# One decoder block on one core: block sums of the output projection on VectorE, and an MLP norm whose row factor is left to the last norm

## The chip, the core and the metric

The kernel runs on one core of a Trainium2 chip. TensorE multiplies, VectorE and ScalarE do the elementwise work, GpSimd does a little of it early on and issues DMAs, SyncE (SP) issues most of the DMAs. DMAs are issued here from SP's, ScalarE's and GpSimd's queues; those that add to what lies at the destination (`accum_op`) all from GpSimd's. Each engine works through its own instructions in order and waits on semaphores for the others. The metric is the device time of one execution in microseconds; a profiled execution gives a trace beside it.

## What is computed

One decoder block on 1024 tokens of width 1024, in float32. The part that matters here is what follows the mixer's two branches (shortened from the reference):

```python
merged = (g_pool * einsum('bsc,cd->bsd', y_pool, w_branch_pool)
          + g_attn * einsum('bsc,cd->bsd', y_attn, w_branch_attn))
mix = einsum('bsd,de->bse', merged, w_out)
x = x + rmsnorm(mix, g_mix_post)
h2 = rmsnorm(x, g_mlp_pre)
ff = einsum('bsf,fd->bsd', square(relu(einsum('bsd,df->bsf', h2, w_up))), w_down)
x = x + rmsnorm(ff, g_mlp_post)      # rmsnorm(v, g) = v * rsqrt(mean(v*v) + 1e-6) * g, by row
```

`relu` squared is homogeneous of degree two, so a factor that a whole row of `h2` carries comes out of `ff` squared, and the last norm divides it out again except in its epsilon.

## The kernel before

**Products.** Each float32 operand is split into a rounded high part (a ScalarE cast) and the rest (a VectorE subtraction); `split` does both, and three matmuls take the place of one (`PASSES`). The large products are done as 2x2 block products by Strassen's scheme in Winograd's form: seven products instead of eight, with sums of blocks as operands. Names such as S1 to S4, A11 to A22 are blocks and block sums of the activations, B11 to B22 and Q1 to Q4 those of the weights, T1 to T4 those of the MLP's activations.

**Pool branch (loop over m = 0 to 7 at L1043).** For each channel block TensorE does 24 matmuls (`mm_fm`, L456 and L458), then `bp_mul` multiplies by the gate and adds the attention branch into the tile `zm[m]`, `bp_split` prepares the next weights, and `merged` splits one half of `zm` as A11 (m < 4) or A12. `merged` also flips signs on ScalarE (`flip`, L956), and `dma_sums` (L979 to L985) forms S1, S2, S3 and S4 in place with DMAs on GpSimd's queue that add one half tile to another. All of GpSimd's other accumulations stand in the same queue: `wo_add` (L1005) adds a block of `w_out` to a weight tile, and L1300 adds one half of an output tile to the other.

**Output projection (L1243 to L1368).** `wo_mm` runs 48 matmuls for one block product, a row block of 128 tokens at a time (t = 0 to 3, 12 matmuls each). TensorE's order is A11·B11, A12·B21, S1·Q1, S2·Q2, S4·B22, S3·Q3, A22·Q4. `s12(k)` splits a whole `zm[k]` as S2 and S1. Q1 is B11 with B12 added to it; after it is split, B22 and later B21 are added to the same tile to give Q2 and Q4. The result of row block n is the tile `ct[n]`: rows 0 to 3 are complete after S4·B22, rows 4 to 7 after A22·Q4.

**Two norms and the residual.** `out_sq`, `root(0)`, `invert(0)` and `out_scale` apply the mixer's post norm; the residual x is added by a DMA on GpSimd's queue (rows 0 to 3, L1138) or by VectorE from a loaded tile (L1140); `nc.sync.dma_start` stores the sum in `x1_dram` on SP's queue. Then `norm_sq`, `root(1)`, `invert(1)` and `norm_scale` apply the MLP's norm in place. `build_first(kt, h)` transposes 128 channels of rows 0 to 3 on TensorE (L1156) and splits them into the MLP's operands; `tr_second` and `build_second` do so for rows 4 to 7.

**MLP.** `Pairs` runs the up projection: for each pair of feature blocks `load` fetches weights, `operand(p, i)` forms and splits the operand of product i, `m1` and `m2` are the first two products, `rest` the other five. Pair p's product 1 therefore needs `operand(p, 1)`, and the call `first_kt(0)` needs `operand(0, 6)` and `operand(0, 7)`. The down projection (L1640 on) runs its products in the order 1, 5, 2, 3, 6, 7, 4, each in 8 steps of 24 matmuls (L1573); `operands` loads and splits two steps ahead, the loaded blocks lying in four buffers (`raw_tile`). `fin_sq`, `add_eps`, `rsqrt_sum` and `fin_out` are the last norm and the last residual, for rows 0 to 3 after product 6 and for rows 4 to 7 after product 4. Its x1 tiles are read from `x1_dram` by `load_x1` and `fin_out`.

**What sets the order.** Inside `tc.manual_schedule(engines=...)` the named engines keep the order in which the program calls them; up to L1304 these are TensorE, VectorE, ScalarE and GpSimd (`MANUAL`), after it only TensorE. For other engines, and SP everywhere here, a planner orders the instructions by program order and by its own estimate of when they are ready. Tiles come from pools with a fixed number of buffers; one that is full makes the next tile's first writer wait. The pool `gp` (`g32`, `gr`) has 17 buffers, `st` (`stage`) has 3, `wp` (`wslot`) has 6.

## Time and profile before

| | us |
|---|---|
| median of 3 runs (lowest, highest) | 1139.15 (1136.72, 1139.19) |
| the profiled execution | 1138.17 |
| its span, first to last instruction | 1136.4 |
| TensorE busy in it | 1103.3 |
| VectorE, ScalarE, GpSimd busy in it | 811.9, 560.1, 67.3 |
| mean granted clock of TensorE | 0.984 |

A row of the timeline gives start, duration, engine, line, operation, what is written from what is read, the shape and the count; in brackets stands the idle time before it and what ended that. A row of the windows gives the stretch and its length, then the busy time and instruction count of TensorE's matmuls, its weight loads, VectorE, ScalarE and GpSimd, then the granted clock, the DMA engines' busy share and GB/s. A row of the groups ends with busy time, mean ns of one, and idle time before. A row of the DMA issues ends with the count, the size of one and the median time from issue to landing. Durations of neighbouring VectorE instructions overlap by a little under 0.1 us, so the distance of two starts is the better price. SP and POOL rows with a queue's DMA show the issue, not the transfer.

### The profile page before, as it was taken

To read this page: it belongs to the slowest core of one execution; us is meant where nothing else is said; L and a number is where in the kernel's file an instruction comes from. 1 tells how busy PE (TensorE), PEld (TensorE's weight loads), DVE (VectorE), ACT (ScalarE), POOL (GpSimd) and SP (SyncE) were. 2 spreads that over 40 slices of the span, in tenths; PEclk is the share of its full clock that TensorE was granted. 3 is DMA by queue.
4 is the path that set the end of the run, shared out by engine and by line. 5 is a ranking of instruction groups with operands and counts; after the bars stand their busy time and mean duration, and the time that the engine had idled before them with its cause. 6 is when DMAs were issued, how large, how long until landed. Compare 5 with 4: busy or idle time off the path is not lost.

```text
span 1136.4 us, 13861 instructions
## 1 busy us (share of the span) xinstructions
PE 1103.3 (97%) x5114; PEld 913.2 (80%) x5114; DVE 811.9 (71%) x1175; ACT 560.1 (49%) x927; POOL 67.3 (6%) x124
## 2 busy tenths in 40 slices
PE   9999999999999995989899999999999999999997
PEld 8888888888888884867688888888888888888886
DVE  6578877998778753857888867575557955446896
ACT  7567665544332443678545544444444345344342
POOL 0433100000001122200000000000000000000000
PEclk9999999999999996989899999999999999999999
DMA  9616465456966777954246634353698765322662
GB/s 347 150 38 190 148 202 201 151 207 205 287 253 167 197 186 158 219 163 163 75 177 216 218 140 185 121 185 121 242 336 296 245 195 191 114 93 74 215 194 92
DMA packets 92531, 208.95 MB, mean 184 GB/s; under 512 B 9520, under 2 KB 22448, under 8 KB 92464
## 3 DMA queue, kind: packets, MB, share of 16 engines
q1 hardware_dynamic: 81072, 176.75, 46.7%
q0 software_dynamic: 5632, 11.54, 5.9%
q10 hardware_dynamic: 5760, 19.79, 4.5%
q8 instruction: 40, 0.66, 0.2%
q14 instruction: 27, 0.22, 0.1%
HBM read 147.23 MB, written 55.58 MB: 178 GB/s over the span
## 4 chain that ended last, share of the span: by engine, by line
PE 86%; DMA 4%; issue 4%; DVE 3%; ACT 2%; POOL 1%; DVEq 0%; POOLq 0%; ACTq 0%
PE mm L520 24%; PE at L520 15%; PE at L1573 14%; PE mm L1573 11%; PE mm L456 4%; PE mm L610 3%; DMA g<-g 2%; PE mm L458 2%; PE mm L192 2%; PE mm L183 2%; PE sc L183 2%; PE sc L429 1%; PE sc L360 1%; DMA qr<-in_w_o_dram 1%; DMA x_dram<-c 1%
## 5 line engine op out<-in xcount | busy, mean ns | idle before, releaser
L1573 PE MATMUL at<-ar,wh 128*128 128x512 f32 x696 | 158.7, 389 | 0.0
L1573 PEld LDWEIGHTS at<-ar,wh 128*128 128x128 f32 x696 | 130.6, 188 | 27.1
L1573 PE MATMUL mm<-ar,wh 128*128 128x512 f32 x576 | 131.0, 389 | 0.0
L1573 PEld LDWEIGHTS mm<-ar,wh 128*128 128x128 f32 x576 | 108.1, 188 | 22.5
L104 DVE TENSOR_TENSOR wh<-raw,wh 128x1024 fp32r<-128x1024 f32 x51 | 62.4, 1224 | 86.0 <-ACT wh L101 85.9
L101 ACT CAST wh<-raw 128x1024 fp32r<-128x1024 f32 x51 | 53.7, 1053 | 132.9 <-PE at L1573 55.2
L101 ACT CAST wh<-st 128x512 fp32r<-128x512 f32 (+1 forms) x104 | 65.4, 642 | 92.3 <-DVE st L499 27.5
L104 DVE TENSOR_TENSOR wh<-st,wh 128x512 fp32r<-128x512 f32 (+1 forms) x105 | 74.4, 720 | 36.2 <-ACT wh L101 33.7
L520 PE MATMUL mm<-gr,wh 128*128 128x512 f32 x333 | 81.4, 396 | 2.3 <-DVE wh L104 2.0
L520 PEld LDWEIGHTS mm<-gr,wh 128*128 128x128 f32 x333 | 63.0, 191 | 16.2 <-DVE wh L104 2.5
L520 PE MATMUL mm<-T,wx 128*128 128x512 f32 x288 | 67.4, 389 | 0.0
L520 PEld LDWEIGHTS mm<-T,wx 128*128 128x128 f32 x288 | 54.1, 188 | 11.2
L520 PE MATMUL at<-T,wx 128*128 128x512 f32 x252 | 58.9, 389 | 0.0
L520 PE MATMUL mm<-x,wh 128*128 128x512 f32 x240 | 55.3, 389 | 0.0
L520 PEld LDWEIGHTS at<-T,wx 128*128 128x128 f32 x252 | 47.3, 188 | 9.8
L520 PEld LDWEIGHTS mm<-x,wh 128*128 128x128 f32 x240 | 45.0, 188 | 9.5 <-DVE z L552 0.2
L610 PE MATMUL mm<-x,wh 128*128 128x512 f32 x192 | 47.8, 395 | 0.0
L104 DVE TENSOR_TENSOR ar<-B,ar 128x1024 fp32r<-128x1024 f32 x37 | 45.2, 1220 | 2.4 <-ACT ar L101 2.0
L610 PEld LDWEIGHTS mm<-x,wh 128*128 128x128 f32 x192 | 35.2, 188 | 7.6 <-DVE qt L104 0.2
L101 ACT CAST ar<-B 128x1024 fp32r<-128x1024 f32 x37 | 38.9, 1051 | 4.7 <-DVE B L1544 2.8
L520 PE MATMUL mm<-T,wh 128*128 128x512 f32 x147 | 38.0, 401 | 3.1 <-ACT wh L101 3.1
L520 PE MATMUL at<-gr,wh 128*128 128x512 f32 x150 | 36.6, 390 | 0.0
(430 smaller groups left out, 2218.2 us busy)
## 6 DMA issues: line engine op xcount, KB each, us to landing
raw<-f_dram SPq DMA_DIRECT2D x53, 512.0 KB, 3.6
f_dram<-g SPq DMA_DIRECT2D x28, 512.0 KB, 3.2
st<-in_w_up_dram SPq DMA_DIRECT2D x24, 512.0 KB, 4.4
B<-in_w_dn_dram SPq DMA_DIRECT2D x24, 512.0 KB, 7.3
st<-in_w_g_dram SPq DMA_DIRECT2D x18, 512.0 KB, 4.1
f_dram<-g ACTq DMA_DIRECT2D x17, 512.0 KB, 2.8
g<-spill_dram SPq DMA_DIRECT2D x16, 512.0 KB, 5.2
raw<-in_w_dn_dram SPq DMA_DIRECT2D x16, 512.0 KB, 4.7
```

Source lines behind the costliest of these rows:

```text
L101: act.copy(hi, src)
L104: eng.tensor_tensor(lo, src, f32(hi), ALU.subtract)
L183: pe.matmul(bq, xs_[k][n // 4][:, xh, n % 4 * P:(n % 4 + 1) * P], wq[k][:, h, :], start=k == 0 and j == 0, stop=k == NK - 1 and j == 2)
L192: pe.matmul(bkv_of(n), xs_[k][n // 4][:, xh, n % 4 * P:(n % 4 + 1) * P], wkv[k // 2][:, h, k % 2, :], start=k == 0 and j == 0 and not (joi ...
L360: pe.matmul(sb[:, kv, i, :nk], qt[r, qx, m * P:(m + 1) * P], kx[r, k0:k0 + nk], start=j == 0, stop=j == 2)
L429: pe.matmul(yb[:, kv], v[:, c:c + P], p[ph][:, 4 * kv:4 * kv + 4].rearrange("p i q -> p (i q)"), start=j < 2, stop=j >= len(mms) - 2)
L456: pe.matmul(bs[th], whi[:, k, :], rhs(k, hl, th), start=k == 0 and hl == 0, stop=False)
L458: pe.matmul(bs[th], wlo[:, k, :], rhs(k, 0, th), start=False, stop=k == nk - 1)
L520: pe.matmul(b, w[:, wh, kt, :], x_, start=not after and kt == 0 and j == 0, stop=kt == 3 and j == 2, skip_group_check=after)
L610: pe.matmul(b, (whi, wlo)[h][:, k, :], xr(k, xh, th), start=j == 0, stop=j == len(mms) - 1)
L1573: pe.matmul(bs[t], fo[fh][:, k2, t * P:(t + 1) * P], wo_[wh][:, k2, :], start=not after and s2 == 0 and k2 == 0 and j == 0, stop=(s2, k2) ...
```

## The change

- The block sums S1 to S4 are formed by VectorE subtractions and additions in `merged` and a new `sum4`; `dma_sums` and the sign flips in `merged` are gone. All four `s12(k)` stand ahead of A12·B21.
- The MLP norm's row factor is not applied. The mixer's post norm scales by r·r1, r1 being the first norm's factor of that row, and the residual comes in as r1·x, so `ct[n]` holds r1·x1. x is always loaded (into the pool `gp`) and added by VectorE; the tile is stored from GpSimd's queue.
- The squares of r1·x1 are taken from memory in product 5 of the down projection; `scaled_eps` forms from them the epsilon that makes the last norm exact, and 1/r1, by which ScalarE scales each x1 tile as it is read. Rows 0 to 3 are finished during product 7.
- The 32 transposes of rows 0 to 3 stand inside A22·Q4, eight behind each row block; operands of pairs 1 and 2 are formed earlier; `operand(0, 6)` and `operand(0, 7)` stand ahead of the third `build_second`, `operand(6, 2)` behind pair 4's second product.

```diff
@@ -966 +966 @@
         if m < 4:
             if m % 2 == 0:
                 s3raw.append(ga_.tile([P, 2, 512], F32, tag="ga", name=nm("s3")))
-            s3 = s3raw[m // 2][:, m % 2, :]
             Am["A11"][m] = split_half(gr, first)
-            flip(s3, second)
-            flip(second, second)
-            nc.gpsimd.dma_start(s3, first, accum_op=ALU.add)
+            dve.tensor_tensor(s3raw[m // 2][:, m % 2, :], first, second, ALU.subtract)
         else:
             k = m - 4
+            s2, s1 = zm[k][:, :512], zm[k][:, 512:]
             Am["A12"][k] = split_half(ar, first)
-            flip(first, first)
-
-    def dma_sums(m):
-        if 0 <= m - 6 < 4:
-            nc.gpsimd.dma_start(zm[m - 2][:, :512], zm[m - 6][:, :512], accum_op=ALU.add)
-        if 0 <= m - 5 < 4:
-            nc.gpsimd.dma_start(zm[m - 5][:, :512], zm[m - 5][:, 512:], accum_op=ALU.add)
-        if 0 <= m - 4 < 4:
-            nc.gpsimd.dma_start(zm[m - 4][:, 512:], zm[m][:, 512:], accum_op=ALU.add)
+            dve.tensor_tensor(s1, second, s1, ALU.subtract)
+            dve.tensor_tensor(s2, s2, s1, ALU.add)
+
+    def sum4(k):
+        first = zm[4 + k][:, :512]
+        dve.tensor_tensor(first, zm[k][:, :512], first, ALU.subtract)
 
     def wo_rows(c, h, j):
         return w_o[4 * h + 2 * c:4 * h + 2 * c + 2].rearrange("k p n -> p k n")[:, :, 512 * j:512 * j + 512]
@@ -1098 +1092 @@
 
...
+    def root(ns):
+        ms = ort[:, 1, ns]
+        dve.scalar_tensor_tensor(ms, osq[:, 0, ns], EPS, osq[:, 1, ns], ALU.add, ALU.add)
+        act.activation(ort[:, 0, ns], ms, AF.Sqrt)
+
+    def invert(ns):
+        s, ms, r, t = (ort[:, i, ns] for i in range(4))
         dve.reciprocal(r, s)
         dve.tensor_tensor(t, r, r, ALU.mult)
         dve.tensor_tensor(t, t, ms, ALU.mult)
+        dve.tensor_tensor(r, r, r1[:, ns], ALU.mult)
         dve.tensor_scalar(t, t, -0.5, 1.5, ALU.mult, ALU.add)
-        dve.tensor_tensor(orr[:, which, ns], r, t, ALU.mult)
+        dve.tensor_tensor(orr[:, ns], r, t, ALU.mult)
 
     xres = {}
 
-    def out_scale(n):
-        t = ct[n]
-        dve.scalar_tensor_tensor(t, t, orr[:, 0, n:n + 1], gpost_b, ALU.mult, ALU.mult)
-        if n < 4:
-            nc.gpsimd.dma_start(t, x[n], accum_op=ALU.add)
-        else:
-            dve.tensor_tensor(t, t, xres.pop(n), ALU.add)
-        nc.sync.dma_start(x1_dram[n], t)
-
-    def norm_scale(n):
-        act.activation(ct[n], ct[n], AF.Identity, scale=orr[:, 1, n:n + 1])
+    def load_res(n):
+        xres[n] = g32([D])
+        nc.sync.dma_start(xres[n], x[n])
+
+    def out_mul(n):
+        dve.scalar_tensor_tensor(ct[n], ct[n], orr[:, n:n + 1], gpost_b, ALU.mult, ALU.mult)
+
+    def out_add(n):
+        dve.scalar_tensor_tensor(ct[n], xres.pop(n), r1[:, n:n + 1], ct[n], ALU.mult, ALU.add)
+        nc.gpsimd.dma_start(x1_dram[n], ct[n])
         hs[n] = ct[n]
-
...
@@ -1265 +1242 @@
             Am["S1"][k] = hi[:, 512:], lo[:, 512:]
 
         b22 = [wo_raw("B22", c, stage) for c in range(2)]
-        s12(0)
-        s12(1)
+        for k in range(4):
+            s12(k)
         up.load(0)
         for t in wo_mm(bm, "A12", "B21", True):
             ct[t] = yy.tile([P, D], F32, tag="y", name=nm("c1"))
@@ -1274 +1251 @@
             if t < 2:
                 wo_split("Q1", t, q1[t], wo_tile)
                 wo_add(q1[t], "B22", t)
-            else:
-                s12(t)
-            if t == 0:
-                dma_sums(9)
+            sum4(t)
         for c in range(2):
             wo_split("B22", c, b22[c], wo_tile)
         ba = [bank("at") for _ in range(4)]
@@ -1302 +1276 @@
             Am["S3"][t] = split_half(gr, s3raw[t // 2][:, t % 2, :])
     with tc.manual_schedule(engines={mybir.EngineType.PE}):
-        load_res(0)
-        load_res(1)
+        for n in range(4):
+            load_res(n)
         for t in wo_mm(ba, "S4", "B22", True):
             dve.tensor_tensor(ct[t][:, 512:], ct[4 + t][:, :512], ba[t], ALU.add)
             out_sq(t, 1)
             if t < 2:
                 wo_split("Q4", t, q1[t], wo_tile)
+            if t == 1:
+                root(p01)
+                up.operand(1, 1)
             if t == 2:
-                root(0, p01)
+                invert(p01)
+                out_mul(0)
+                out_add(0)
             if t == 3:
-                invert(0, p01)
-                out_scale(0)
-                load_res(2)
-                root(0, p23)
-                out_scale(1)
-                load_res(3)
-                invert(0, p23)
+                root(p23)
+                out_mul(1)
+                out_add(1)
+        up.load(4)
         bm = [bank("mm") for _ in range(4)]
         for t in wo_mm(bm, "S3", "Q3"):
-            if t == 1:
-                norm_sq(0)
-                norm_sq(1)
-                out_scale(2)
-                up.load(4)
-                root(1, p01)
-            if t == 2:
-                out_scale(3)
-                load_res(4)
-                load_res(5)
-                norm_sq(2)
-                invert(1, p01)
-                norm_scale(0)
-                norm_scale(1)
-            if t == 3:
-                norm_sq(3)
-                root(1, p23)
-                invert(1, p23)
-                norm_scale(2)
-                norm_scale(3)
+            if t == 0:
+                invert(p23)
+                for n in range(4, 8):
+                    load_res(n)
             u = ct[4 + t]
             dve.tensor_tensor(u[:, 512:], u[:, 512:], bm[t], ALU.add)
             out_sq(4 + t, 1)
-        up.operand(1, 1)
-        up.operand(1, 2)
-        up.operand(2, 1)
-        up.operand(2, 2)
+            if t < 2:
+                out_mul(2 + t)
+                out_add(2 + t)
+            else:
+                up.operand(t - 1, 4 - t)
         for t in wo_mm(bm, "A22", "Q4", True):
             u = ct[4 + t]
             dve.tensor_tensor(u[:, :512], u[:, :512], bm[t], ALU.add)
             out_sq(4 + t, 0)
+            for kt in range(2):
+                build_first(t % 2 * 2 + kt, t // 2)
+            if t == 1:
+                root(p45)
+                up.operand(2, 2)
             if t == 2:
-                for kt in range(4):
-                    build_first(kt, 0)
-        root(0, p45)
-        invert(0, p45)
-        out_scale(4)
-        load_res(6)
-        out_scale(5)
-        load_res(7)
-        norm_sq(4)
-        norm_sq(5)
-        root(0, p67)
+                invert(p45)
+                out_mul(4)
+                out_add(4)
+            if t == 3:
+                root(p67)
+                out_mul(5)
+                out_add(5)
     opool.__exit__(None, None, None)
 
 
@@ -1399 +1362 @@
 
 
     with tc.manual_schedule(engines={mybir.EngineType.PE}):
-        invert(0, p67)
+        invert(p67)
+        for n in (6, 7):
+            out_mul(n)
+            out_add(n)
         up.m1(0, bank("mm"))
-        root(1, p45)
-        for kt in range(4):
-            build_first(kt, 1)
-        out_scale(6)
-        out_scale(7)
         up.m1(1, bank("mm"))
-        invert(1, p45)
-        norm_scale(4)
-        norm_scale(5)
         up.load(6)
         up.load(8)
         up.load(10)
-        norm_sq(6)
-        norm_sq(7)
-        root(1, p67)
-        invert(1, p67)
-        norm_scale(6)
-        norm_scale(7)
         up.operand(3, 1)
         up.operand(3, 2)
         up.m1(2, bank("mm"))
@@ -1441 +1393 @@
         m1_late(5)
         tr = tr_second(2)
         up.operand(6, 1)
-        up.operand(6, 2)
+        up.operand(0, 6)
+        up.operand(0, 7)
         build_second(2, *tr)
         up.m2(3)
         tr = tr_second(3)
         build_second(3, *tr)
         m1_late(6)
-        up.operand(0, 6)
-        up.operand(0, 7)
         up.m2(4)
+        up.operand(6, 2)
         for kt in range(4):
             build_last(kt)
         up.operand(0, 5)
@@ -1576 +1528 @@
 
     def fin_sq(n, dj, v):
 
-        act.activation(junk, v, AF.Square, scale=ROOT_D, accum_out=sq[:, dj, n:n + 1])
+        squared.append(act.activation(junk, v, AF.Square, scale=ROOT_D, accum_out=sq[:, dj, n:n + 1]))
...
+    squared = []
+
+    def read_x1(n, t):
+        nc.sync.dma_start(flat(t), x1_dram[n])
+        with tc.issue_after(squared[-1].ins):
+            act.activation(flat(t), flat(t), AF.Identity, scale=ort[:, 4, n:n + 1])
+        xf[n] = t
+
     def load_x1(n):
-        t = rp.tile([P, 2, 512], F32, tag="w", name=nm("xf"))
-        nc.sync.dma_start(flat(t), x1_dram[n])
-        xf[n] = t
+        read_x1(n, rp.tile([P, 2, 512], F32, tag="w", name=nm("xf")))
+
+    def square_x1(n):
+        t = flat(raw_tile())
+        nc.sync.dma_start(t, x1_dram[n])
+        act.activation(t, t, AF.Square, scale=ROOT_D, accum_out=nsq[:, n:n + 1])
+
+    def scaled_eps():
+        q = ort[:, 5, :]
+        dve.reciprocal(ort[:, 4, :], r1)
+        dve.tensor_tensor(q, r1, r1, ALU.mult)
+        dve.scalar_tensor_tensor(q, q, EPS, nsq, ALU.mult, ALU.add)
+        dve.scalar_tensor_tensor(ort[:, 6, :], q, EPS, q, ALU.mult, ALU.mult)
 
     def add_eps(ns, dj):
-        dve.tensor_scalar(sq[:, dj, ns], sq[:, dj, ns], EPS, None, ALU.add)
+        dve.tensor_tensor(sq[:, dj, ns], sq[:, dj, ns], ort[:, 6, ns], ALU.add)
 
     def fin_out(n, hv):
         if n not in xf:
-            t = stage([2, 512])
-            nc.sync.dma_start(flat(t), x1_dram[n])
-            xf[n] = t
+            read_x1(n, stage([2, 512]))
         for dj in (1, 0):
             o = xf[n][:, dj, :]
             dve.scalar_tensor_tensor(o, hv[dj][n % 4], rr[:, n:n + 1], o, ALU.mult, ALU.add)
@@ -1656 +1624 @@
             tag = "mm" if i in (5, 7) else "at"
             banks[i] = [bank(tag) for _ in range(4)]
         bs = banks[{2: 1, 3: 5}.get(i, i)]
+        if i == 5:
+            square_x1(s_)
+        if i == 7 and 1 <= s_ <= 4:
+            fin_out(s_ - 1, (c11, c12))
         if i != 4 or s_ < NS - LATE:
             down_mm(i, s_, bs, i in (2, 3), [(s_, k2, t) for k2 in range(2) for t in range(4)
                                              if (i, s_, t) != (4, NS - LATE - 1, 3)])
@@ -1701 +1673 @@
                 fin_gain(0, c11[t], u[t])
                 rsqrt_sum(rr[:, n:n + 1], sq[:, 0, n:n + 1], sq[:, 1, n:n + 1])
                 fin_out(n, (c11, v))
+        if i == 2:
+            scaled_eps()
         if i == 7:
             add_eps(slice(4, NT), 1)
             for n in range(4, NT):
@@ -1708 +1682 @@
         if i == 6:
             add_eps(slice(0, 4), 1)
             rsqrt_sum(rr[:, 0:4], sq[:, 0, 0:4], sq[:, 1, 0:4], 4)
-            for n in range(4):
-                fin_out(n, (c11, c12))
     rpool.__exit__(None, None, None)
 
 
```

More of the change, by code (lines that the diff above doesn't have):

```diff
@@ L1055, in block_kernel @@
                 merged(m - 1)
-                dma_sums(m - 1)
             if m in (4, 5):
@@ L1100, in block_kernel @@
     nsq = sp.tile([P, NT], F32, tag="nsq", name="nsq", bufs=1)
-    orr = sp.tile([P, 2, NT], F32, tag="orr", name="orr", bufs=1)
-    ort = sp.tile([P, 6, NT], F32, tag="ort", name="ort", bufs=1)
+    orr = sp.tile([P, NT], F32, tag="orr", name="orr", bufs=1)
+    ort = sp.tile([P, 7, NT], F32, tag="ort", name="ort", bufs=1)
     def out_sq(n, h):
@@ L1276, in block_kernel @@
                 wo_add(q1[t], "B22", t)
-            else:
-                s12(t)
-            if t == 0:
-                dma_sums(9)
+            sum4(t)
         for c in range(2):
```

22 lines of the change are left out of this document (2 added, 20 removed).

## The prediction

> **What bounds the kernel now.** I read the head of the page first (busy time and clock), then the waits of TensorE, then TensorE in order of time around each wait, then the engine that each wait names.
>
> ```profile
> span 1136.4 us, 13861 instructions
> PE 1103.3 (97%) x5114; PEld 913.2 (80%) x5114; DVE 811.9 (71%) x1175; ACT 560.1 (49%) x927; POOL 67.3 (6%) x124
> PE at L1095 <- ACT gr L101: 13.5, 1, 13.5
> PE at L1156 <- ACT c L1144: 5.0, 2, 4.5
> PE mm L520 <- ACT wh L101: 3.4, 2, 3.1
> PE mm L520 <- DVE wh L104: 2.0, 1, 2.0
> ```
>
> TensorE is busy for 97% of the span, so a gain can only come out of the other 33 us or out of time in which it ran slowly. The four waits shown (line, who released, total, times, longest) are nearly all the idle time in the middle of the kernel. The same places in order of time, one window for each stretch; the column after the engines is the granted clock:
>
> ```profile
> 425.66:439.15 13.49, 0.00 (x1) 0.00 (x0) 0.02 (x1) 1.09 (x2) 5.01 (x5) 0.59 0.67 113
> 439.15:445.20 6.05, 6.00 (x13) 4.29 (x14) 5.31 (x5) 3.89 (x5) 1.36 (x2) 0.51 1.00 205
> 496.86:503.20 6.34, 5.77 (x20) 4.99 (x21) 4.30 (x10) 5.61 (x12) 0.00 (x0) 0.50 0.01 3
> 551.49:559.12 7.63, 7.63 (x19) 5.30 (x20) 6.43 (x9) 3.23 (x5) 0.00 (x0) 0.59 0.39 132
> 867.80:911.32 43.52, 43.52 (x193) 36.04 (x193) 40.00 (x35) 18.21 (x21) 0.00 (x0) 1.00 0.70 234
> 517.80 6.41 PE L520 MATMUL mm<-gr,wh 128*128 128x512 f32 x27 [2.01 <-DVE wh L104]
> 551.49 2.75 PE L520 MATMUL mm<-T,wh 128*128 128x512 f32 x5 [3.08 <-ACT wh L101]
> ```
>
> After a long wait the clock stands at half for some 6 us. At full clock the row from 867.80 gives 43.52 / 192 = 0.227 us a matmul (one of the 193 begins in the next product). So a wait has two prices:
> - Q1 wait: 13.49 idle, then 13 matmuls in 6.05 instead of 2.95: 16.6 us.
> - First transposes: 5.05 idle (the wait row), then half of 5.77 busy at clock 0.50: 7.9 us.
> - Up projection, pair 3: 2.0 and a neighbour of 0.3 (the rest of the 3.4): 2.3 us. No row shows a lower clock after it.
> - Up projection, product 6 of pair 0: 3.08 idle, then 19 matmuls in 7.63 instead of 4.31: 6.4 us.
>
> Together 33.2 us, the most that this change can bring. Everything behind 559 us is TensorE back to back, and the last few us are the final norm's short chain.
>
> The largest wait, at its source: ScalarE could not cast the third row block of the sums, and GpSimd's queue shows why.
>
> ```profile
> 438.06 1.04 ACT L101 CAST gr<-g 128x1024 fp32r<-128x1024 f32 x1 [13.80 <-DMA g<-g]
> 417.87 0.87 POOL L983 DMA_DIRECT2D g<-g  x1 [6.90 <-DMA g<-g]
> 422.19 1.21 POOL L1005 DMA_DIRECT2D qr<-in_w_o_dram  x1 [2.56 <-PE mm L1095]
> 428.48 1.21 POOL L1005 DMA_DIRECT2D qr<-in_w_o_dram  x1 [5.08 <-issue]
> 434.68 0.89 POOL L983 DMA_DIRECT2D g<-g  x1 [4.06 <-issue]
> DMA to landing us min/median/max: 4.0/6.0/9.2
> ```
>
> The sum of line 983 that the cast needs is issued at 434.68, behind two weight accumulations that each hold the queue 6.3 us (422.19 to 428.48). The last row is the landing time of those accumulations (the tile qr).
>
> **The change part by part.**
>
> *Block sums on VectorE.* Gone: 16 accumulating DMAs and 12 sign flips on ScalarE. Added: 16 VectorE operations on 128x512.
>
> ```profile
> 457.41 0.68 DVE L1299 TENSOR_TENSOR c<-c,mm 128x512 f32<-128x512 f32 x1
> 458.01 0.69 DVE L104 TENSOR_TENSOR gr<-s,gr 128x512 fp32r<-128x512 f32 x1
> L1029 DVE TENSOR_TENSOR g<-g,g 128x1024 f32<-128x1024 f32 x6 | 7.4, 1226 | 0.2
> ```
>
> Successive starts are 0.60 apart, 1.14 for the wide form (1.23 less the same overlap of 0.09). Each channel block of the pool branch takes 24 matmuls, 5.44 us. VectorE's work in the fullest of them (m = 5) becomes 2.3 (gate products and sum) + 0.6 (weight split) + 1.8 (one split and two sums) + 1.1 (B11 split) = 5.8 us; it overruns by 0.4 in two blocks and recovers in the next, and the weights for the next block are split before the overrun. I take nothing; without that order it is at most 2 x 0.4.
>
> ```profile
> 401.70 0.39 PE L1095 MATMUL mm<-B11h,gr 128*128 128x512 f32 x1
> ```
>
> The last block's products end where this first output product starts, 401.7; 2.3 and 1.8 later, by 406, all sums for S1 and S2 are there, and their casts begin behind the copies of the first product, at 413. So the Q1 wait goes: -16.6 us.
>
> What is late next is Q2, because its weights are Q1's, accumulated in place after Q1 was split. If TensorE does not stop, the products (48 matmuls, 10.88 us each) start at 401.7 (A11), 412.6 (A12), 423.5 (S1), 434.3 (S2), 445.2 (S4), 456.1 (S3) and 467.0 (A22).
>
> ```profile
> 417.25 1.23 DVE L104 TENSOR_TENSOR Q1l<-qr,Q1h 128x1024 fp32r<-128x1024 f32 x1
> 442.25 1.05 ACT L101 CAST Q2h<-qr 128x1024 fp32r<-128x1024 f32 x1
> ```
>
> Q1's first split ended at 418.5; now two more block splits go ahead of it, so about 420.6. The first accumulation is issued then, the second 6.3 later at 426.9, it lands 6.0 later at 432.9, cast and subtraction take 1.05 + 1.23: 435.2. S2 reaches this half at its seventh matmul, 435.9. At the median nothing is lost; with 9.2 twice it is 420.6 + 9.2 + 9.2 + 2.3 = 441.3, a wait of 5.4 and half clock after it, 3.1: 8.5 us. ScalarE's copies and A22 casts lie between, so I take +0.5, bounds 0 to 8.5. [...]
>
> Behind it in GpSimd's queue are Q4's two accumulations (issued at 433.2 and 439.5, needed at 467), then four small ones of line 1300 from 446; the last lands near 455, before S3's first tile at 459.
>
> *Mixer norm, residual, no MLP row factor.* Gone from ScalarE, and from the chain ahead of the transposes:
>
> ```profile
> L1144 ACT ACTIVATE c<-c,orr 128x1024 f32<-128x1024 f32 x8 | 8.8, 1141 | 2.0 <-DMA x_dram<-c 1.6 <-DVE orr L1130 0.4
> L1109 ACT ACTIVATE junk_b<-c 128x1024 f32<-128x1024 f32 x8 | 8.5, 1061 | 6.6 <-DMA c<-in_x_dram 6.5
> c<-in_x_dram POOLq DMA_DIRECT2D x4, 512.0 KB, 7.0
> st<-in_x_dram SPq DMA_DIRECT2D x8, 512.0 KB, 5.1
> ```
>
> The old chain was scale, accumulate x by DMA (7.0), store, square, root, scale; the new one is scale and one multiply-add with x loaded ahead. The eight x loads (5.1 each) stay on SP but go to the 17-buffer pool, where buffers come free when S2 ends (445 us); with 6 to 10 us for the first four together they are there between 451 and 455, and row block 0 needs its own at 457. The stores of x1 leave SP for GpSimd behind line 1300, and nobody reads them before the down projection. SP's queue, in which the load for pair 3 sat behind those stores, is freed.
>
> ```profile
> 477.55 2.48 DVE L1136 SCALAR_TENSOR_TENSOR c<-c,orr,bc 128x1024 f32<-128x1024 f32 x2
> 471.90 0.16 DVE L1126 RECIPROCAL sm<-ort 128x2 f32<-128x2 f32 x1
> 472.89 1.29 DVE L1136 SCALAR_TENSOR_TENSOR c<-c,orr,bc 128x1024 f32<-128x1024 f32 x1
> 512.76 2.06 DVE L1167 SCALAR_TENSOR_TENSOR gr<-at,snk,gr 128x512 fp32r<-128x512 f32 x3
> 525.64 1.03 PE L1156 MATMUL at<-cst,c 128*128 128x128 f32 x8
> 504.62 2.89 PE L520 MATMUL mm<-gr,wh 128*128 128x512 f32 x12
> ```
>
> VectorE pays 1.24 a row block for each of the two steps, and six dependent small operations for a root (five took 472.89 - 471.90 = 1.0, so 1.2). From S4's second tile (452 us): four tile additions and one operand split 3.0, two roots 2.4, four row blocks 9.9, with S3's first two additions 1.2: 16.5, so rows 0 to 3 are ready near 468.5. The first transposes stand behind A22's first tile, at 467.0 + 2.7 = 469.7. Margin 1 us: the 7.9 go; the other end is 3 us of wait, should VectorE start late.
>
> *Order around the transposes.* All 32 transposes of rows 0 to 3 now stand in A22 (0.9 us for each eight), so A22 runs from 467 (467.5 with the Q2 wait) to 482 and the first products of pairs 0, 1, 2, 3 follow at 2.72 each (pair 0 started at 504.62 before, with half the transposes still to come): pair 3 at 490.2. VectorE is at 468.5 + four more 0.60 (two additions of S3, two operand splits) = 470.9 when it turns to A22, and then has four additions 2.4, eight build steps at 0.69 = 5.5, two roots 2.4, four row blocks 9.9, operand (2,2) 0.6: 20.8, to 491.8, and only then pair 3's subtraction, 0.6: 492.4. TensorE waits about 2.2 where it waited 2.3. Bounds: 0 if the subtraction goes ahead of row blocks 6 and 7, which nothing needs before the transposes near 500; and 9.3 if VectorE comes 4 us later still (6.2 idle and 3.1 of half clock). I take +2.2.
>
> *Product 6 of pair 0.* Its operand, late by 3.08 before, goes ahead of two transposed builds that took VectorE 4.4 us each; the displaced builds and operand (6,2) are needed only 3 to 6 us later. VectorE has no norm work left here. The 6.4 go; if operand (6,2), whose buffer is freed by pair 4's second product, is late instead, 0.6 to 3 come back.
>
> *Down projection.* Added: eight x1 loads and ScalarE squares in product 5 (1.06 and 0.19 for the readout), eight scalings by 1/r1 later (1.14 each), rows 0 to 3 finished during product 7. In product 5's window above ScalarE works 18.2 of 43.5 us, so 10 us more fit. But each step now takes two of four load buffers, so a block can be loaded two steps ahead instead of four.
>
> ```profile
> B<-in_w_dn_dram SPq DMA_DIRECT2D x24, 512.0 KB, 7.3
> raw<-f_dram SPq DMA_DIRECT2D x53, 512.0 KB, 3.6
> ```
>
> Two steps are 10.9 us; the slowest of these rows, 7.3, plus cast and subtraction, 2.3, is 9.6. It fits; I take 0.
>
> **Sum.** 1138.2 (the profiled execution; span 1136.4) - 16.6 - 7.9 - 2.3 - 6.4 + 0.5 + 2.2 = 1107.7. The median of the runs shown is 1.0 above that execution, so the forecast is 1109.
>
> **Rivals.**
> 1. *Q2's accumulations take the place of the sums.* For it: 0.7 us of slack and landings up to 9.2. Against: the queue no longer carries anything else. 8.5 instead of 0.5: 1117.
> 2. *VectorE becomes the bound in S4 to A22.* For it: it takes over 16 sums, eight residual additions and gives up nothing large there, and my margins are 1 to 2 us. Against: in the same stretch ScalarE loses 17 us, on which VectorE used to wait. 9.3 instead of 2.2: 1116.
> 3. *The sums were not what held Q1.* Then the 16.6 stay, 1125. The rows against it: cast, DMA and queue name the same transfer.
> 4. *Slower: the load buffers in product 5.* If the x1 loads and squares share the four buffers so that only one block load is in flight, a step is 7.3 + 2.3 = 9.6 instead of 5.44: 8 x 4.2 = 33 more, 1142, and more with the clock. It decides from landings above 8.6 us (10.9 - 2.3) and turns the sign when a step grows by 30 / 8 = 3.8 us. For it: the loads add 4.2 MB in 43.5 us, 96 GB/s to 234. Against: ScalarE's casts there come two steps ahead of use.
>
> **How the numbers follow.** Forecast 0.66, rival 1 0.12, rival 2 0.11, rival 3 0.03, rival 4 0.08. The predicted time is the forecast's. All waits gone is 1138.2 - 33.2 + 1.0 = 1106, and the runs shown lie up to 2.4 under their median: low end 1103. Rivals 1 and 2 with some of each other's price end at 1122. What is left out is rivals 3 and 4, about 0.1. A measurement of this kernel tells a difference from about 0.3%, 3.4 us: faster 0.90 (forecast, rivals 1 to 3, less a remainder), same 0.02, slower 0.08.
>
> **What would show it.** Right: no wait of S1 for a cast released by a DMA; no clock of 0.5 between 425 and 445; the first transposes without a wait; the first products of the pairs near 482 instead of 504; product 5 without a gap. Wrong: a wait of S2 released by the cast or split of Q2 (rival 1), waits on VectorE with that engine full from 452 to 495 (rival 2), gaps in product 5 with loads above 8.6 us (rival 4). The prediction fails if new waits add up to more than 13 us.

## The result and the profile after

The changed kernel takes 1107.77 us (median of 4 runs, 1105.71 to 1107.95) against 1138.71 for the kernel before on the same chip (4 runs, 1136.72 to 1139.19): a ratio of 0.9727, 95% interval 0.9711 to 0.9744. The forecast was 1109 in a range of 1103 to 1122.

The busy times in the head of the page of the changed kernel:

```profile
PE 1095.2 (99%) x5114; PEld 909.4 (82%) x5114; DVE 822.8 (74%) x1179; ACT 551.8 (50%) x911; POOL 54.2 (5%) x112
```

And all its waits of TensorE (line, who released, total, times, longest); the span is 1106.0 us:

```profile
PE mm L201 <- DVE pad L160: 1.1, 1, 1.1
PE mm L1089 <- ACT Q2h L101: 1.0, 1, 1.0
PE mm L1089 <- DVE Q2l L104: 0.8, 1, 0.8
PE sc L403 <- DVE s L369: 0.5, 1, 0.5
```

The four waits of before, 13.5, 5.0, 3.4 and 2.0, are gone. The 1.1 and 0.5 lie outside the changed stretch. What is new is 1.8 us for the second half of Q2. TensorE's busy time fell too, by 8.1 us for the same 5114 matmuls: that is mostly time at the clock of 0.50 to 0.59 in three windows of the prediction, which no longer occurs. The same engine in order of time, at the places of the steps:

```profile
436.98 0.50 PE L1089 MATMUL mm<-Q2h,gr 128*128 128x512 f32 x1 [1.02 <-ACT Q2h L101]
438.24 0.50 PE L1089 MATMUL mm<-Q2l,gr 128*128 128x512 f32 x1 [0.76 <-DVE Q2l L104]
...
473.79 1.03 PE L1135 MATMUL at<-cst,c 128*128 128x128 f32 x8
...
485.42 16.58 PE L520 MATMUL mm<-gr,wh 128*128 128x512 f32 x72
...
524.45 1.52 PE L520 MATMUL mm<-T,wh 128*128 128x512 f32 x6
...
837.25 43.68 PE L1525 MATMUL mm<-ar,wh 128*128 128x512 f32 x192
```

A row without brackets had no idle time in front of it. S1 runs through. Q2's wait is the only one. The first transposes (473.79), the first products of the pairs from 485.42 on (72 in one row, so pair 3 among them), product 6 of pair 0 (524.45) and product 5 of the down projection (837.25) start without a wait.

The wait at its source, GpSimd's queue and ScalarE's cast:

```profile
421.13 1.21 POOL L1000 DMA_DIRECT2D qr<-in_w_o_dram  x1 [12.71 <-DVE Q1l L104]
427.13 1.21 POOL L1000 DMA_DIRECT2D qr<-in_w_o_dram  x1 [4.79 <-DMA qr<-in_w_o_dram]
426.62 1.46 SPq L483 DMA_DIRECT2D st<-in_w_up_dram  x2
435.88 1.04 ACT L101 CAST Q2h<-qr 128x1024 fp32r<-128x1024 f32 x1 [5.58 <-DMA qr<-in_w_o_dram]
```

The accumulations are issued at 421.13 and 427.13 (predicted: 420.6 and 426.9). The second releases the cast at 435.88, 8.7 us after its issue, where the median before was 6.0. On SP's queue two loads of up-projection weights are issued beside it, at 426.62 and 427.76. Two rows of the windows, one behind this wait and one for product 5 (columns as before):

```profile
440.00:445.00 5.00, 5.00 (x18) 3.94 (x17) 4.99 (x9) 5.00 (x13) 2.13 (x2) 0.71 0.42 70
837.25:880.77 43.52, 43.52 (x194) 36.04 (x192) 33.25 (x30) 27.00 (x37) 0.00 (x0) 1.00 0.85 298
```

Behind Q2's wait the granted clock is 0.71 over 5 us (0.51 from 440 to 443, 1.00 from 443 to 445), a loss of 5 x 0.29 = 1.45; from 436 to 440 it is 0.94, another 0.24. So Q2 costs 1.8 idle and 1.7 of clock, 3.5. In product 5 ScalarE is at 27.0 of 43.5 us, and TensorE is at 0.227 us a matmul as before.

### The profile page after: what moved, and what is told of

The parts are those of the page before. It is cut to its first block, busy times and chain, and to the rows that moved or that the text cites. A ratio compares the mean times of both kernels' runs of the same rounds, so it can differ in the third digit from the quotient of the medians.

```text
span 1106.0 us, 13829 instructions
## 1 busy us (share of the span) xinstructions
PE 1095.2 (99%) x5114; PEld 909.4 (82%) x5114; DVE 822.8 (74%) x1179; ACT 551.8 (50%) x911; POOL 54.2 (5%) x112
## 4 chain that ended last, share of the span: by engine, by line
PE 92%; DVE 3%; issue 2%; ACT 1%; DMA 1%; POOL 0%; DVEq 0%; POOLq 0%; ACTq 0%
PE mm L520 26%; PE at L520 16%; PE at L1525 15%; PE mm L1525 12%; PE mm L456 4%; PE mm L610 3%; PE mm L1089 3%; PE mm L458 2%; PE mm L192 2%; PE sc L183 2%; PE mm L183 2%; PE sc L429 1%; PE sc L360 1%; PE at L1089 1%; DMA qr<-in_w_o_dram 1%
```

## The experiments

Twelve kernels ran in three groups of four, beside the kernel before on their chip (medians 1141.89, 1139.97 and 1139.47). Ratios are to that; spans are compared to show where the time lies (before 1136.4, changed 1106.0). The kernel before itself is up to 3.2 us slower on these chips than beside the changed kernel, and the changed kernel was not run in these groups. A difference of spans of 3 us or less therefore counts only where the trace shows the wait or the clock that makes it.

**e1: the sums alone.** The kernel before with the block sums on VectorE and all `s12` ahead of A12·B21; norms and orders as before.

```diff
-            flip(s3, second)
-            flip(second, second)
-            nc.gpsimd.dma_start(s3, first, accum_op=ALU.add)
+            dve.tensor_tensor(s3raw[m // 2][:, m % 2, :], first, second, ALU.subtract)
...
-        s12(0)
-        s12(1)
+        for k in range(4):
+            s12(k)
```

> The kernel before with one part of the change: block sums by VectorE, all four S1/S2 splits ahead of A12. Theory (four separate waits): the Q1 wait and its slow clock go, -16.6, and the Q2 wait of the changed kernel appears (1.8 idle and 1.7 of half clock, +3.5); the other three waits stay: 1138.7 - 13.1 = 1125.6. Rival (the rest of the stage is late anyway): TensorE comes 13 us earlier to the transposes, whose norm chain of ScalarE and DMA is not earlier, so the first-transposes wait grows by most of the gain: 1132 to 1138.

Measured: 1125.75 us, ratio 0.9853 (0.9837 to 0.9870), span 1124.8. Its waits of TensorE:

```profile
PE at L1150 <- ACT c L1138: 4.6, 2, 4.0
PE mm L520 <- ACT wh L101: 3.4, 2, 3.1
PE mm L1089 <- ACT Q2h L101: 2.6, 1, 2.6
PE mm L520 <- DVE wh L104: 2.0, 1, 2.0
PE mm L1089 <- DVE Q2l L104: 0.8, 1, 0.8
```

The wait of 13.5 is gone, the three others stay, and Q2 takes 3.4 back, with a clock of 0.66 from 440 to 445 behind it. By the terms that is 16.6 - 3.4 - 1.7 = 11.5, and the span is 11.6 shorter. Against the kernel before in its own group, which is slower, the gain is 16.1 us, so the agreement of the total to 0.1 is partly luck; the trace shows which waits went and which stayed. Sums and norms are separate gains, as predicted.

**e2: everything but the sums.** The changed kernel with `flip`, `dma_sums` and the old places of `s12` back.

```diff
-            dve.tensor_tensor(s3raw[m // 2][:, m % 2, :], first, second, ALU.subtract)
+            flip(s3, second)
+            flip(second, second)
+            nc.gpsimd.dma_start(s3, first, accum_op=ALU.add)
...
-            sum4(t)
+            else:
+                s12(t)
+            if t == 0:
+                dma_sums(9)
```

> The changed kernel with the block sums and sign flips back on DMAs and ScalarE, norm and order as changed. Theory: the Q1 wait returns (13.5 idle, 3.1 of half clock) and the Q2 wait of 3.5 goes, since Q1's split is then long done when S2 starts: 1107.8 + 16.6 - 3.5 = 1120.9. Rival (norm and order need the earlier sums): later operands of S4 and A22 bring back a wait at the transposes as well, 1128 or more.

Measured: 1122.97 us, ratio 0.9832 (0.9815 to 0.9849), span 1120.8. Its largest wait:

```profile
PE at L1095 <- ACT gr L101: 13.9, 1, 13.9
```

The old wait is back at the old place, for the same cast; Q2's falls to 0.3 and no other of the four returns. Rival 3 (the sums did not hold Q1) falls on both sides.

**e4: Q1 split first.** The changed kernel with the splits of Q1 and the accumulations behind them ahead of the four `s12`.

```diff
+        for t in range(2):
+            wo_split("Q1", t, q1[t], wo_tile)
+            wo_add(q1[t], "B22", t)
         for k in range(4):
             s12(k)
...
-            if t < 2:
-                wo_split("Q1", t, q1[t], wo_tile)
-                wo_add(q1[t], "B22", t)
             sum4(t)
```

> The changed kernel with the two Q1 splits and the accumulations that follow them ahead of the four S1/S2 splits. Theory (the Q2 wait comes from the length of the chain Q1 split, accumulate, accumulate, split): the chain starts 4 to 5 us earlier, both Q2 halves are ready by 432, both waits of S2 and the half clock after them go: 1107.8 - 3.5 = 1104.3. Rival 1 (S1's operands become late): S1 waits 1 us or more for the last S2/S1 split, 1106 to 1109. Rival 2 (the landing grows by what else moves then): the second landing stays late and the time stays at 1107.8.

Measured: 1104.27 us, ratio 0.9673 (0.9656 to 0.9689), span 1102.3. The accumulations are issued 4.0 and 2.7 us earlier than in the changed kernel, and the second cast comes 5.5 earlier:

```profile
417.10 1.21 POOL L1000 DMA_DIRECT2D qr<-in_w_o_dram  x1 [7.36 <-DVE Q1l L104]
424.44 1.21 POOL L1000 DMA_DIRECT2D qr<-in_w_o_dram  x1 [6.13 <-DMA qr<-in_w_o_dram]
430.33 1.05 ACT L101 CAST Q2h<-qr 128x1024 fp32r<-128x1024 f32 x1 [0.71 <-DVE ar L104]
```

Only 2.7 of the 5.5 are the earlier issue. The second accumulation also lands faster, at most 5.9 us after its issue (the cast at 430.33 waits for VectorE) instead of 8.7, although the same two loads of up-projection weights still run beside it: here they are issued about 1.5 and 2.6 us behind it (the later at 427.1; the earlier at 425.94, an estimate from the 1.14 between the two in the changed kernel), where in the changed kernel one was issued 0.5 ahead of it and one 0.6 behind. Q2's wait and the low clock are gone (its matmuls start 0.227 us apart from 433.75 on), 3.7 us in the span. The interval lies below that of the changed kernel (0.9711 to 0.9744), so this version beats the change as it was made, as far as ratios from two chips can be compared.

**e9: the loads held back.** The changed kernel with `up.load(2)` and `up.load(4)` on SP behind the first four loads of x.

```diff
-        up.load(2)
...
         for n in range(4):
-            load_res(n)
+            held = load_res(n)
+        with tc.issue_after(held.ins):
+            up.load(2)
...
-        up.load(4)
+        with tc.issue_after(held.ins):
+            up.load(4)
```

> The changed kernel with the weight loads of pairs 1 and 2 held on SP until the first four x loads are issued, so that no load runs beside the second Q2 accumulation (issued at 427.1, landed at 435.9 in the changed kernel, with two weight loads issued at 426.6 and 427.8). Theory (contention of transfers made the 6.0 of the sum into 8.7): it lands in about 6.0, at 433.1, cast and subtraction end at 435.4, S2 does not wait: 1104.3 to 1105. Rival (the accumulation is that slow by itself): it lands in 8 to 9 us again and the time stays at 1107.8.

Measured: 1108.26 us, ratio 0.9705 (0.9691 to 0.9720), span 1106.5.

```profile
428.13 1.21 POOL L1000 DMA_DIRECT2D qr<-in_w_o_dram  x1 [5.12 <-DMA qr<-in_w_o_dram]
433.93 1.05 ACT L101 CAST Q2h<-qr 128x1024 fp32r<-128x1024 f32 x1 [2.97 <-DMA qr<-in_w_o_dram]
457.45 0.69 DVE L104 TENSOR_TENSOR wh<-st,wh 128x512 fp32r<-128x512 f32 x1 [4.14 <-ACT wh L101]
472.55 0.33 PE L1135 MATMUL at<-cst,c 128*128 128x128 f32 x1 [1.71 <-DVE c L1126]
473.75 0.77 PE L1135 MATMUL at<-cst,c 128*128 128x128 f32 x5 [0.87 <-DVE c L1126]
```

The second accumulation lands at most 5.8 us after its issue instead of 8.7, and Q2's wait is gone: the loads beside it had made it late. But the span does not fall (the ratio is 0.2% lower than the changed kernel's, with intervals that overlap; e4, in the same group, is 4.0 us faster). VectorE sits idle for 4.14 us ahead of 457.45, for ScalarE's cast of weights that the held loads bring late. Row block 3 is complete 1.8 us later for it, and the first transposes wait 2.6 us. The loads were only put from one margin into another; e4 wins because it moves the accumulations instead.

**e3: product 6's operand late again.**

```diff
-        up.operand(0, 6)
-        up.operand(0, 7)
+        up.operand(6, 2)
         build_second(2, *tr)
...
         m1_late(6)
+        up.operand(0, 6)
+        up.operand(0, 7)
         up.m2(4)
-        up.operand(6, 2)
```

> The changed kernel with one move undone: product 6's operand (0,6),(0,7) goes behind m1_late(6) again, and operand (6,2) behind operand (6,1). The changed kernel's span is 1106.0 us. Theory (my prediction's step: the move bought the 6.4 us): TensorE stops about 3 us before product 6 of pair 0 and runs at half clock behind it, span about 1112. Rival (the norm's leaving VectorE bought it, the move adds nothing): in the changed kernel the transposed builds in front of it begin some 8 us earlier than TensorE needs this operand, so with the old order there is a wait of 0 to 1.5 us and no half clock: span 1106 to 1107.5.

Measured: 1114.19 us, ratio 0.9779 (0.9763 to 0.9795), span 1112.7.

```profile
522.78 0.68 DVE L492 TENSOR_TENSOR ws<-st 128x512 f32<-128x512 f32 x1
526.49 0.62 ACT L101 CAST wh<-ws 128x512 fp32r<-128x512 f32 x1
527.15 2.75 PE L520 MATMUL mm<-T,wh 128*128 128x512 f32 x5 [3.08 <-ACT wh L101]
```

The wait is the 3.08 of before, to the hundredth, with a lower clock behind it (0.84 from 520 to 530, 0.82 from 530 to 540). The span is 6.7 longer although this execution lost no clock at Q2 (1.00 from 425 to 445). The rival, that the norm's leaving had already freed VectorE, is wrong: in the old order the first step of that operand stands behind two transposed builds and starts at 522.78, while in the changed kernel it starts at 512.11.

**e7 and e7b: the row factor kept.** The changed kernel, new order included, with the MLP norm's row factor applied and without the squares of x1 in product 5.

```diff
+        act.activation(junk_b, ct[n], AF.Square, scale=ROOT_D, accum_out=nsq[:, n:n + 1])
...
+    nrt = sp.tile([P, 4, NT], F32, tag="nrt", name="nrt", bufs=1)
+    nrr = sp.tile([P, NT], F32, tag="nrr", name="nrr", bufs=1)
...
+            act.activation(ct[n], ct[n], AF.Identity, scale=nrr[:, n:n + 1])
...
-        if i == 5:
-            square_x1(s_)
```

> The changed kernel with the MLP norm's row factor applied again to rows 0 to 7 (square and scale on ScalarE, six small VectorE operations and a root for each two rows), and so without the squares of x1 in product 5; everything else, the new order too, stays. Theory (dropping the factor is what frees the first transposes): row 3 was there at 471.9 and TensorE wanted it at 473.8; square 1.06, root about 1.7 and two scales 2.3 make it 477, so a wait of about 3 us with 1.7 to 3 us of lower clock behind it, and VectorE's 4.8 us more between 460 and 495 may bring back pair 3's wait of 2: span 1110 to 1114. Rival (the early x loads and the one-step residual are what freed them): 0 to 1 us, span 1106 to 1107.

Measured: 1137.66 us, ratio 0.9975 (0.9965 to 0.9985), span 1136.4. That is 22 us above the theory's range, and not where either looked: the transposes wait 7.8 us, but TensorE is also busy 22.3 us longer than in the changed kernel. Its busy times, then groups (the last number but one is the mean of one in ns), then a window of the down projection:

```profile
PE 1117.5 (98%) x5114; PEld 912.7 (80%) x5114; DVE 825.7 (73%) x1201; ACT 560.1 (49%) x923; POOL 54.1 (5%) x112
```

```profile
L1545 PE MATMUL at<-ar,wh 128*128 128x512 f32 x696 | 164.0, 396 | 0.0
L520 PE MATMUL mm<-gr,wh 128*128 128x512 f32 x333 | 81.7, 397 | 0.0
L520 PE MATMUL mm<-T,wx 128*128 128x512 f32 x288 | 67.6, 390 | 0.0
```

```profile
900.00:1000.00 100.00, 100.00 (x428) 80.42 (x427) 48.95 (x44) 43.56 (x56) 0.00 (x0) 1.00 0.50 155
```

The changed kernel starts 443 matmuls in that window, 0.227 us apart, and e7 428, at clock 1.00 in both. The first two groups have a mean of 389 and 391 there, the third 389. What the slow groups share is tiles that lie behind the new scratch in memory (`ar`, `gr`), read together with one whose place did not change (`wh`). So e7b has the same instructions and only gives the scratch 256 bytes instead of 160 (`[P, 7, NT]` for `[P, 4, NT]`):

> The kernel of e7_factor_kept once more (the MLP norm's row factor applied, no squares of x1 in product 5), with one thing changed: its added scratch takes 256 bytes a partition instead of 160. In e7 the matmuls that read one tile behind the scratch and one ahead of it (ar with wh, gr with wh, T with ar) started 0.233 us apart instead of 0.227 at a granted clock of 1.00, while those that read two tiles of one side (T with wx, gr with ar) kept 0.227. Theory (the 160 bytes moved one of the two operands off the other's alignment, and the row factor itself costs only its waits, some 8 us with the lower clock behind them): all matmuls are 0.227 apart again and the span is 1113 to 1118. Rival (the row factor's work slows the matmuls in some other way): 0.233 again, span 1134 to 1138.

Measured: 1122.11 us, ratio 0.9848 (0.9820 to 0.9877), span 1119.4, 1.4 us above the theory's range and far from the rival's. Busy times and waits:

```profile
PE 1097.9 (98%) x5114; PEld 910.8 (81%) x5114; DVE 825.7 (74%) x1201; ACT 559.9 (50%) x923; POOL 54.2 (5%) x112
```

```profile
PE at L1150 <- ACT c L1142: 9.0, 6, 4.0
PE mm L1089 <- ACT Q2h L101: 1.7, 1, 1.7
```

19.6 us of busy time are gone again with 96 bytes. What is left is the price of the row factor in the new order: 13.4 us over the changed kernel, of which 9.0 are idle time at the transposes, 2.7 busy time, with the matmuls behind them 0.43 us apart from 482.5 to 485.1, 0.7 more wait at Q2 and 0.8 a wait in the down projection.

**e10 and e11: the address alone.** The changed kernel with an unused tile behind the scratch of the output norm, and not one instruction more.

```diff
     ort = sp.tile([P, 7, NT], F32, tag="ort", name="ort", bufs=1)
+    sp.tile([P, 8], F32, tag="shift", name="shift", bufs=1)
```

> The changed kernel with nothing but an unused tile of 32 bytes a partition added behind the output norm's scratch, which moves the tiles ar, gr, g and raw by 32 bytes and leaves wh, T, wx and x. No instruction is added. Theory (two operands of a matmul at different offsets within 64 bytes cost 3%): the matmuls of the down projection, 0.227 us apart in the changed kernel, are 0.233 apart, and with those of the projection and the pair products, some 2,600 in all, the span is 17 to 25 us longer, 1123 to 1131. Rival (addresses do not matter, e7's slower matmuls came from elsewhere): 1105.5 to 1106.5.

> As e10_shift32, with 64 bytes instead of 32. If what counts is the offset within 64 bytes, nothing changes: 1105.5 to 1106.5. If it is the offset within 128 or 256 bytes, or the distance itself, it is as slow as e10, 1123 to 1131, or slower.

Measured: e10 1124.69 us, ratio 0.9863 (0.9839 to 0.9887), span 1122.9; e11 (16 for 8 in the added line) 1115.94 us, ratio 0.9790 (0.9765 to 0.9815), span 1115.8. Busy times of e10, then of e11:

```profile
PE 1112.1 (99%) x5114; PEld 908.5 (81%) x5114; DVE 823.4 (73%) x1179; ACT 551.9 (49%) x911; POOL 54.1 (5%) x112
```

```profile
PE 1104.9 (99%) x5114; PEld 909.0 (81%) x5114; DVE 823.7 (74%) x1179; ACT 551.8 (49%) x911; POOL 54.1 (5%) x112
```

TensorE is busy 16.9 us longer with 32 bytes (0.1 below the expected 17) and 9.7 longer with 64 (in the slowest of e11's four executions, 1.6 above their median); the waits stay within 0.4 of the changed kernel's. In the window from 900 to 1000 they start 431 and 439 matmuls at clock 1.00, where the changed kernel starts 443. So an address alone cost 1.5% in e10 (16.9 of 1106.0 us). That the offset within 64 bytes is what counts was the author's guess, and e11 speaks against it: 64 bytes cost 9.7, more than half of the 16.9 of 32, and 256 (e7b) nothing that can be seen (443 matmuls in the same window). The other branch, as slow as e10 or slower, did not come either.

**e8: the transposes in their old places.**

```diff
-            for kt in range(2):
-                build_first(t % 2 * 2 + kt, t // 2)
...
             if t == 2:
+                for kt in range(4):
+                    build_first(kt, 0)
...
         up.m1(0, bank("mm"))
+        for kt in range(4):
+            build_first(kt, 1)
```

> The changed kernel with the transposes of rows 0 to 3 in their old places: sixteen behind A22's third tile and sixteen behind the first product of pair 1, instead of eight behind each of four tiles. Theory (the order is worth nothing once the row factor is gone, since row 3 is there 1.9 us before the first transposes): the same within 1 us, span 1105 to 1107. Rival (the order is a part of the gain): sixteen transposes in one go need VectorE's or ScalarE's copies faster than they come, or the first product waits for its operand: 2 us or more, span 1108 to 1112.

Measured: 1113.53 us, ratio 0.9771 (0.9757 to 0.9786), span 1111.6: the rival. TensorE, then VectorE around the wait:

```profile
496.04 10.87 PE L520 MATMUL mm<-gr,wh 128*128 128x512 f32 x34 [3.22 <-DVE wh L104]
488.54 2.48 DVE L1123 SCALAR_TENSOR_TENSOR c<-c,orr,bc 128x1024 f32<-128x1024 f32 x2
490.94 2.48 DVE L1126 SCALAR_TENSOR_TENSOR c<-g,r,c 128x1024 f32<-128x1024 f32 x2
493.33 2.06 DVE L1146 SCALAR_TENSOR_TENSOR gr<-at,snk,gr 128x512 fp32r<-128x512 f32 x3
495.31 1.88 DVE L104 TENSOR_TENSOR wh<-st,wh 128x512 fp32r<-128x512 f32 x3
```

The transposes do not wait, but pair 3 does, for a subtraction that stands behind row blocks 6 and 7 and three builds. Its 3.22 and the lower clock behind it (0.79 from 492 to 508, 3.4 us) make 6.6, and three more short waits 1.1. The span is only 5.6 longer because this execution lost no clock at Q2 (1.00 from 436 to 445), where the changed kernel lost 1.7.

**e12: the stores of x1 on SP.**

```diff
-        nc.gpsimd.dma_start(x1_dram[n], ct[n])
+        nc.sync.dma_start(x1_dram[n], ct[n])
```

> The changed kernel with the stores of x1 on SP's queue as before, instead of GpSimd's. Theory (my prediction's step: SP, in which pair 3's load sat behind the stores, had to be freed): each store waits on SP for its row block, so the loads behind it start up to 10 us late, and pair 3 or pair 4 waits 2 to 6 us: span 1108 to 1112. Rival (the rows are now ready earlier than the loads are needed, so the queue does not matter): span 1105.5 to 1106.5.

Measured: 1107.09 us, ratio 0.9723 (0.9702 to 0.9743), span 1105.1: no price. SP's queue did not have to be freed. Pair 3 starts without a wait here too, and the 0.9 by which the span is shorter is explained by the low clock behind Q2's wait (0.71 from 440 to 445), which this execution does not have (1.00; last section).

**e6: twice the added loads in product 5.**

```diff
-            square_x1(s_)
+            for _ in range(2):
+                square_x1(s_)
```

> The changed kernel with the loads and squares of x1 in product 5 done twice each (the second overwrites the first's sum with the same value): 16 loads and 16 squares where the change added 8. Theory (my prediction took 0 for these: ScalarE works 18 of 43.5 us there and the load buffers leave two steps): the same within 0.5 us if a step has room left, span 1105.5 to 1107; with three loads a step on four buffers little room is left, so up to 5 us would still not speak against the 0 for the single one. Rival (rival 4 of the prediction, the load buffers bind): a step grows from 5.44 to 7 to 10 us, 12 to 36 us in all, span 1118 to 1142.

Measured: 1108.17 us, ratio 0.9728 (0.9701 to 0.9754), span 1106.7. The 0.7 us lie at Q2, where this execution waited 1.7 instead of 1.0; TensorE's busy time is the changed kernel's 1095.2. Eight more loads and squares cost nothing in product 5, so the eight of the change do not either, and rival 4 falls.

## Why the prediction held, point by point

| term | predicted | measured | shown by |
|---|---|---|---|
| Q1 wait and clock | -16.6 | gone | e1 (-11.6 with Q2's 5.1 against it), e2 (13.9 back) |
| first transposes | -7.9 | gone | e7b: 9.0 idle at them with the factor |
| product 6 of pair 0 | -6.4 | gone | e3: back, 3.08 idle, 6.7 longer span |
| pair 3, old wait | -2.3 | gone | e8: 3.22 back with the old order |
| pair 3, new wait | +2.2 | 0 | row from 485.42 |
| Q2's accumulations | +0.5 | +3.5 | rows at 436.98 and 438.24; e4, e9 |
| down projection | 0 | 0 | e6 |

With the measured terms the sum is 1138.2 - 33.2 + 3.5 = 1108.5; the profiled execution took 1107.8.

**Q2, mis-sized.** The two issue times were right to 0.5 us and TensorE's need (435.9) too. What failed is "it lands 6.0 later": with two loads of up-projection weights issued within 0.7 us of it, it took 8.7. The median had been taken over transfers with other neighbours. e9 shows these loads to be the cause (without them it landed in at most 5.8), and e4 that their moment counts: issued about 1.5 and 2.6 us behind the accumulation, they left its landing at 5.9 or less. Why the moment counts is not shown. Rival 1 named this place with 8.5 us from two slow landings; one was slow. So a sign of rival 1 came (S2 waits for the cast and the split of Q2), and a sign of being right did not (the clock is 0.51 from 440 to 443), but at 3.5 instead of 8.5 us.

**Pair 3, mis-sized.** "And only then pair 3's subtraction" was the branch that did not occur. VectorE in the changed kernel:

```profile
492.32 0.68 DVE L104 TENSOR_TENSOR wh<-st,wh 128x512 fp32r<-128x512 f32 x1
...
493.31 2.48 DVE L1123 SCALAR_TENSOR_TENSOR c<-c,orr,bc 128x1024 f32<-128x1024 f32 x2
```

The planner put the subtraction ahead of row blocks 6 and 7, the case given as the lower bound. In e8 it put it behind them, and the wait came, 3.22 us with a clock of 0.79 from 492 to 508, as in the upper one. The two errors, -2.2 and +3.0, nearly cancel, so the total is better than its parts.

**The first transposes, right in mechanism.** The chain on VectorE from S4's second tile to the end of row block 3 was put at 16.5 us (452 to 468.5). The changed kernel:

```profile
455.31 0.68 DVE L1285 TENSOR_TENSOR c<-c,at 128x512 f32<-128x512 f32 x1
469.42 2.48 DVE L1126 SCALAR_TENSOR_TENSOR c<-g,r,c 128x1024 f32<-128x1024 f32 x2
```

It took 16.6, to 471.9. Both ends came some 3.4 us later than predicted, but TensorE too came 4.1 later, most of it by Q2: it wanted row block 3 at 473.8 instead of 469.7. So the margin is 1.9 us where 1 was predicted.

**Right, but for one reason too many.** The prediction let the freed SP queue help pair 3; e12 shows that it had no part. It also gave the order around the transposes nothing beyond its terms for pair 3; e8 puts that order at 5.6 us, and e7b shows that dropping the factor is worth 13.4 in it, more than the 7.9 read off the kernel before, whose transposes stood later.

**Not thought of.** The change takes 32 bytes a partition (8 floats) from `orr`, `[P, 2, NT]` to `[P, NT]`, and gives 32 to `ort`, `[P, 6, NT]` to `[P, 7, NT]`, so the tiles behind them stay where they were. A net shift of 32 bytes cost 16.9 us in e10, half the gain.

## What to carry to other kernels

Price a transfer that becomes critical by its landing with the neighbours that it will have and the moment at which they are issued, not by its median (here 8.7 us with two loads issued within 0.7 us of it and at most 5.8 without them, where the median was 6.0), and look for the cheapest way to issue it earlier before moving the neighbours (e4 against e9). A wait that ends on a planner's choice deserves both branches in the sum. Where a variant is slower with full clock and no new wait, count matmuls in equal windows and see whether a tile's address moved, before any mechanism is believed (428 in e7 against 443 in e7b, from 900 to 1000).

## What the runs showed of the hardware

**Addresses.** Moving the tiles `ar`, `gr`, `g`, `raw` and all others behind the scratch by 32, 64 or 160 bytes, with `wh`, `T`, `wx` and `x` in place, made TensorE busy for 16.9, 9.7 and, against e7b, 19.6 us more, with the granted clock at 1.00 from 900 to 1000 in each; 256 bytes did not (443 matmuls in that window, as in the changed kernel). In e7 matmuls whose operands both stayed in place (`T` with `wx`) lost 1 ns of 389, those whose operands both moved (`gr` with `ar`) 2, and those with one moved operand 6 (`gr` with `wh`, of 391) or 7 (`ar` with `wh`), which points to the distance of the two operands. In e11 it is less clear: `ar` with `wh` in the down projection and `T` with `wx` both stand at 391, 2 more than in the changed kernel, and `gr` with `wh` at 393, also 2 more. Whether that distance decides or what the other engines read and write at the same time was not told apart.

**The clock after short waits.** The same wait, Q2's, had different ends. The window from 440 to 445 in e3, then in e12, against the row of the changed kernel above:

```profile
440.00:445.00 5.00, 5.00 (x24) 4.09 (x23) 4.98 (x9) 5.00 (x13) 1.22 (x1) 1.00 0.52 90
```

```profile
440.00:445.00 5.00, 5.00 (x23) 4.13 (x22) 4.98 (x9) 5.00 (x12) 1.92 (x2) 1.00 0.44 72
```

Q2's two pieces were 1.3 and 0.8 us in e3, 0.9 and 0.8 in e12, 1.0 and 0.8 in the changed kernel: 2.1 and 1.7 left the clock at 1.00, 1.8 brought it to 0.71. In e10 the same 1.3 and 0.8 as in e3 came with a clock of 0.96 from 400 to 445, a loss of 1.8 us. The 2.6 of e9 at the transposes left it at 1.00 (425 to 480) too. So, between these 1.7 and 2.6 us, the length alone does not decide; what else does was not shown. In a sum for this kernel such a wait cost its own length or some 1.7 us more.
